# A diffusion trunk's two attentions written as three-part steps, issued on TensorE in a fixed staggered order

## The chip, the cores and the metric

The kernel runs on one core of a Trainium2 chip. The metric is device time in microseconds of one execution. A core has TensorE (PE; its weight loads are listed as PEld), VectorE (DVE), ScalarE (ACT), GpSimd (POOL) and SyncE (SP), which issues the transfers here. Each engine takes its instructions in the order in which they stand in its own queue, and waits on semaphores for the others.

## What is computed

One step of a small diffusion trunk of two layers. 640 tokens go through each layer: 512 latent tokens and 128 prompt tokens. A layer is a feed-forward half step, a mixer and another feed-forward half step. The mixer has three parts on the same input, whose outputs are concatenated and projected: multi-head latent attention (MLA, 8 heads, all keys), window attention with a sink (SWA, 8 query heads on 2 key heads, a band of three blocks of 128 plus 128 cached tokens), and a gated delta network run in both directions (GDN, 4 heads). Prompt tokens attend to the 128 prompt tokens only.

```python
def mla_attend(q_nope, q_rope, k_nope, k_rope, v):
    scale = (MLA_NOPE + MLA_ROPE) ** -0.5
    def one(qs):                       # a block of 128 queries
        qn, qr = qs
        s = (jnp.einsum('bqhd,bshd->bhqs', qn, k_nope)
             + jnp.einsum('bqhr,bsr->bhqs', qr, k_rope)).astype(jnp.float32) * scale
        p = jax.nn.softmax(s, axis=-1).astype(v.dtype)
        return jnp.einsum('bhqs,bshd->bqhd', p, v)
...
def swa_band_attend(q, k, v, k_ctx, v_ctx, sink):
...
    s_loc = jnp.where(valid[None, :, None, None], s_loc, -jnp.inf)
    s_ctx = jnp.einsum('bnqkgd,blkd->bnkgql', qb, k_ctx).astype(jnp.float32) * scale
...
    p = jax.nn.softmax(jnp.concatenate([s_loc, s_ctx, snk], axis=-1), axis=-1)
...
def mixer_latent(h, lp, ctx):
...
    o_gdn, _ = gdn_bidirectional(pr, lp, st_c[:, 0], st_c[:, 1])
    out = jnp.concatenate([o_mla, o_swa, o_gdn], axis=-1) @ lp['w_out']
...
def macaron_layer(x, mod, lp, mix_fn):
    x = x + g1 * (0.5 * swiglu(modulate(rms_norm(x, lp['norm_ffn1']), sh1, sc1), lp['ffn1_w1'], lp['ffn1_w2']))
    m, aux = mix_fn(modulate(rms_norm(x, lp['norm_mix']), sh2, sc2))
    x = x + g2 * m
    x = x + g3 * (0.5 * swiglu(modulate(rms_norm(x, lp['norm_ffn2']), sh3, sc3), lp['ffn2_w1'], lp['ffn2_w2']))
    return x, aux
```

## The kernel before

All of it is float32; large matrix products run as three products of a high and a low part (`linear`, line 104). Activations stand transposed, features on partitions. The mixer of a layer (`mixer`, from line 315) works in this order:

- The input projections and the four GDN heads of the latent tokens (`gdn_group`, groups 0 to 3), then `project`, which makes MLA's queries, keys and values and writes them to DRAM. The four heads of the prompt form a fifth group.
- A GDN group has a preparation: norm sums (line 615), transposes and Gram matrices in PSUM banks of the kind G, a triangular inverse of 16 x 16 blocks on VectorE in 15 dependent rounds (lines 692 to 694), and the block products (line 703), which alternate with VectorE. A scan follows: two directions, eight steps each, of a matmul at line 742, one at line 745, and VectorE's updates (lines 743, 746), in one bank each, S0 and S1.
- Window attention, `swa` (line 946). For a head and a block of 128 queries: scores into an S bank (line 981, masks line 985; the prompt's block line 1006), then `finish` (line 898): the maximum on VectorE (905), the bias (907 or 909), the exponential on ScalarE (910), for SWA the sink's exponential and its sum (912, 913), the reciprocal (914) and the scaling on GpSimd (915). Then `pv` (line 918): 128 x 128 transposes on TensorE into T banks (931), copies by ScalarE (938), products with the values (942), and the output's copy (944). Query blocks go in pairs, since their products share the values.
- MLA, `mla` (line 1011): the same with 640 columns of scores per block (line 1036, six matmuls each), five pairs of transposes and five products of 256 columns per pair of blocks. A head is two pairs and the prompt's block. After head 0 the fifth group's output is normed and written (`tail`, in two pieces).
- After two MLA heads the pool of GDN is given back and the outputs that lie in DRAM are loaded again and split into high and low parts (`osplit`; tile `of`, line 67 on ScalarE). Then come the output projection and the residual.

PSUM has eight banks. During the projections they are L 4, G 2, S0 1, S1 1; in window attention S 2 and T 2 take the place of L, and G, S0 and S1 stay; in MLA S has two tiles of two banks and T four.

The order on every engine is a scheduler's: it simulates the program as it is written and lets each engine take what is ready. So in window attention TensorE's queue mixes scores, transposes and products with the fifth group's preparation and with two scans.

Of the kernel before, what the change touches and what calls it, by code (L numbers as in the profile page):

```python
# [11 lines left out]
AX = mybir.AxisListType  # L12
PSUM = bass.MemoryType.PSUM
# [28 lines left out]
class Net:  # L42
# [272 lines left out]
    def mixer(self, l, A, B, G):  # L315
# [5 lines left out]
        self.enter_banks(G=2, S0=1, S1=1, side="right")  # L321
# [174 lines left out]
        with self.pool("wo") as wp:  # L496
            o = {}

            def osplit(i, f):
                hi = wp.tile([P, T], F32R, tag="o", name=self.nm("oh"), bufs=24)  # L500
                lo = wp.tile([P, T], F32R, tag="o", name=self.nm("ol"), bufs=24)
                self.split(f, hi, lo)
                o[i] = (hi, lo)

            for i in (8, 9, 10, 11, 4, 5, 6, 7, *range(1)):
                f = wp.tile([P, T], F32, tag="of", name=self.nm("of"), bufs=2)
                nc.sync.dma_start(f, self.do[i])
                osplit(i, f)
            self.mla(l, range(2, 8), wp, osplit)
            self.leave_banks()  # L510
            acm.__exit__(None, None, None)
            self.hp_open()
            self.open_x()
            for k in range(KD):
                nc.sync.dma_start(self.x[k], self.xd[k])
            with self.banks(L=6, G=2):
                order = (8, 9, 10, 11, 4, 5, 6, 7, 0, 1, 2, 3)
                for n in range(KD):
                    w = self.weight(a['wo'][l, n, :, 8:], 4, P) + self.weight(a['wo'][l, n, :, :8], 8, P)
                    w = w[:4] + w[8:] + w[4:8]  # L520
                    self.residual(n, w, [o[i] for i in order], G, True)
# [396 lines left out]
    def pv(self, blocks, vv, o, r0, c0, width):  # L918
# [17 lines left out]
        for p, used in tiles:  # L936
            f = self.att.tile([P, 512], F32, tag="pt", name=self.nm("pt"), bufs=6)
            nc.scalar.activation(f[:, :used], p[:, :used], AF.Copy)
            hl.append(f)
        po = self.pt("T")  # L940
# [4 lines left out]

    def swa(self, l):
        nc, att = self.nc, self.att
        sink = self.sm(l, 'sink')
        for kv in range(2):
# [8 lines left out]
            for hh in range(4):  # L958
                head = kv * 4 + hh
                r0 = 64 * (head % 2)  # L960
                if hh % 2 == 0:
                    ot = att.tile([P, T], F32, tag="out", name=self.nm("out"), bufs=2)
                qh = att.tile([P, T], F32R, tag="q", name=self.nm("q"), bufs=4)
                for n in range(2):
                    self.move(qh[64 * n:64 * n + 64], self.dsq[head // 2][n][r0:r0 + 64])
                fin = lambda p, w: self.finish(p[:, :w].unsqueeze(1), SC_SWA, -SC_SWA, self.nsink[:, l * 8 + head:l * 8 + head + 1], sink[:, head:head + 1])

                def scores(n):
                    q = slice(n * P, (n + 1) * P)
                    p = self.pt("S")  # L970
                    lo, hi_ = max(0, n - 1), min(4, n + 2)
                    nl = hi_ - lo
                    if n >= 2:
                        rng = [(0, lo * P, T - lo * P)]
                    else:
                        rng = [(0, 0, nl * P), (nl * P, TL, P)]
                    k = 0
                    last = 2 * len(rng) + (n > 0) + (n < 3)
                    for o0, k0, w in rng:
                        for x in (kh, kl):  # L980
                            nc.tensor.matmul(p[:, o0:o0 + w], lhsT=qh[:, q], rhs=x[:, k0:k0 + w], start=(k == 0), stop=(k == last - 1))  # L981
                            k += 1
                    for on, o0, m in ((n > 0, 0, 'msw1'), (n < 3, (nl - 1) * P, 'msw2')):
                        if on:
                            nc.tensor.matmul(p[:, o0:o0 + P], lhsT=self.identb, rhs=self.mask[m], start=False, stop=(k == last - 1))
                            k += 1
                    return p, (nl + 1) * P, lo, nl

                for pair in range(2):
                    info = []  # L990
                    for n in (2 * pair, 2 * pair + 1):
                        p, w, lo, nl = scores(n)
                        info.append((fin(p, w), lo, nl))
                    blocks = [(4, [(info[j][0], info[j][2] * P, j) for j in range(2)])]
                    single = []
                    for b in range(4):
                        parts = [(info[j][0], (b - info[j][1]) * P, j) for j in range(2)
# [276 lines left out]
```

## Time and profile before

| | us |
|---|---|
| median of three runs (3323.11 to 3327.07) | 3326.66 |
| the profiled execution | 3325.07 |
| its span | 3323.3 |
| window attention, layer 0 (first score to first MLA score) | 111.35 |
| MLA, layer 0 (to the output projection) | 105.64 |
| window attention, layer 1 | 110.00 |
| MLA, layer 1 | 106.63 |

The page lists busy time by engine; a matmul's end is modelled, and short ones overlap, so starts are a better measure of them than durations. A view by stretches gives busy time and the granted clock of TensorE within bounds. A time line lists what an engine ran, neighbours of one kind merged, with the idle time ahead of it in brackets and what ended it.

### The profile page before, as it was taken

To read this page: it belongs to the slowest core of one execution; us is meant where nothing else is said; L and a number is where in the kernel's file an instruction comes from. 1 tells how busy PE (TensorE), PEld (TensorE's weight loads), DVE (VectorE), ACT (ScalarE), POOL (GpSimd) and SP (SyncE) were. 2 spreads that over 40 slices of the span, in tenths; PEclk is the share of its full clock that TensorE was granted. 3 is DMA by queue.
4 is the path that set the end of the run, shared out by engine and by line. 5 is a ranking of instruction groups with operands and counts; after the bars stand their busy time and mean duration, and the time that the engine had idled before them with its cause. 6 is when DMAs were issued, how large, how long until landed. Compare 5 with 4: busy or idle time off the path is not lost.

```text
span 3323.3 us, 56733 instructions
## 1 busy us (share of the span) xinstructions
PE 3241.5 (98%) x22036; PEld 3129.5 (94%) x22036; DVE 1886.3 (57%) x4357; ACT 1384.8 (42%) x3041; POOL 452.2 (14%) x480
## 2 busy tenths in 40 slices
PE   8999999999998999999999999999999989999998
PEld 5999999999887999999999999999998879999998
DVE  4564577686885355643346735477878653433333
ACT  3332334554676433322233323255466763321222
POOL 0000011222343100100000100012114340000000
PEclk9999999999999999999999999999999999999999
DMA  6443453322714224522224534333235242222222
GB/s 212 128 149 116 134 164 127 97 76 91 201 54 138 84 86 133 155 94 72 69 92 143 156 99 139 98 103 110 72 121 152 75 138 74 69 73 74 83 65 76
DMA packets 180190, 364.78 MB, mean 110 GB/s; under 512 B 28112, under 2 KB 68176, under 8 KB 179920
## 3 DMA queue, kind: packets, MB, share of 16 engines
q1 hardware_dynamic: 179920, 361.15, 35.2%
q8 instruction: 173, 2.83, 0.4%
q14 instruction: 97, 0.79, 0.1%
HBM read 315.03 MB, written 46.04 MB: 109 GB/s over the span
## 4 chain that ended last, share of the span: by engine, by line
PE 87%; DVE 6%; ACT 3%; DMA 2%; issue 2%; SPq 0%; POOL 0%; POOLq 0%; DVEq 0%; ACTq 0%
PE psL L104 72%; PE psT L942 3%; PE psG L703 3%; PE psS L1036 2%; PE psT L931 1%; PE psG L275 1%; PE psS L742 1%; DMA of<-do 1%; PE psS L745 1%; ACT pr L910 1%; PE psS L981 1%; DVE hf L169 1%; DMA adaw<-in_wada_dram 0%; DVE wlo L70 0%; PE psS L776 0%
## 5 line engine op out<-in xcount | busy, mean ns | idle before, releaser
L70 DVE TENSOR_TENSOR wlo<-wr,whi 128x512 fp32r<-128x512 f32 (+2 forms) x726 | 494.2, 682 | 709.5 <-ACT whi L67 708.0
L67 ACT ACTIVATE whi<-wr 128x512 fp32r<-128x512 f32 (+2 forms) x726 | 446.2, 616 | 876.2 <-PE psL L104 614.9
L104 PE MATMUL psL<-hb,whi 128*128 128x320 f32 x1968 | 523.8, 313 | 0.7 <-DVE hb L171 0.5
L104 PE MATMUL psL<-hc,whi 128*128 128x320 f32 x1952 | 521.0, 314 | 0.0
L104 PE MATMUL psL<-ha,whi 128*128 128x320 f32 x1856 | 492.3, 312 | 5.0 <-DVE ha L171 3.7
L104 PE MATMUL psL<-hd,whi 128*128 128x320 f32 (+1 forms) x1856 | 486.3, 310 | 1.9 <-DVE hd L171 1.9
L104 PE MATMUL psL<-mh,wlo 128*128 128x320 f32 x1408 | 434.2, 309 | 0.0
L104 PE MATMUL psL<-ml,whi 128*128 128x320 f32 x1408 | 434.0, 309 | 0.0
L104 PE MATMUL psL<-mh,whi 128*128 128x320 f32 x1408 | 432.9, 310 | 0.0
L104 PEld LDWEIGHTS psL<-hb,whi 128*128 128x128 f32 x1968 | 351.9, 189 | 2.6 <-DVE hb L171 1.2
L104 PEld LDWEIGHTS psL<-hc,whi 128*128 128x128 f32 x1952 | 349.4, 189 | 0.8
L104 PEld LDWEIGHTS psL<-ha,whi 128*128 128x128 f32 x1856 | 329.8, 188 | 8.6 <-DVE ha L171 5.7
L104 PEld LDWEIGHTS psL<-hd,whi 128*128 128x128 f32 (+1 forms) x1856 | 328.9, 188 | 5.2 <-DVE hd L171 3.1
L269 DVE SCALAR_TENSOR_TENSOR ada<-adaw,cs,ada 128x512 f32<-128x512 f32 x448 | 313.7, 743 | 0.0
L104 PE MATMUL psL<-hb,wlo 128*128 128x320 f32 (+1 forms) x984 | 307.3, 312 | 0.0
L104 PE MATMUL psL<-hc,wlo 128*128 128x320 f32 (+1 forms) x976 | 305.6, 313 | 0.0
L104 PE MATMUL psL<-hd,wlo 128*128 128x320 f32 (+1 forms) x928 | 287.7, 310 | 0.0
L104 PE MATMUL psL<-ha,wlo 128*128 128x320 f32 (+1 forms) x928 | 287.5, 311 | 0.0
L104 PEld LDWEIGHTS psL<-ml,whi 128*128 128x128 f32 x1408 | 264.0, 188 | 2.8
L104 PEld LDWEIGHTS psL<-mh,whi 128*128 128x128 f32 x1408 | 263.5, 188 | 3.0
L104 PEld LDWEIGHTS psL<-mh,wlo 128*128 128x128 f32 x1408 | 264.1, 188 | 2.0
L273 POOL TENSOR_TENSOR adal<-ada,adah 128x512 fp32r<-128x512 f32 x64 | 89.8, 1404 | 1041.7 <-ACT adah L67 823.3
(299 smaller groups left out, 5612.1 us busy)
## 6 DMA issues: line engine op xcount, KB each, us to landing
adaw<-in_wada_dram SPq DMA_DIRECT2D x288, 256.0 KB, 2.9
wr<-in_w1a_dram SPq DMA_DIRECT2D x88, 512.0 KB, 3.7
wr<-in_w1b_dram SPq DMA_DIRECT2D x88, 512.0 KB, 3.5
wr<-in_win_dram SPq DMA_DIRECT2D x54, 512.0 KB, 3.5
wr<-in_w2a_dram SPq DMA_DIRECT2D x32, 512.0 KB, 4.0
wr<-in_w2b_dram SPq DMA_DIRECT2D x32, 512.0 KB, 3.5
wr<-in_wo_dram SPq DMA_DIRECT2D x16, 512.0 KB, 3.6
dqn<-hd SPq DMA_DIRECT2D x24, 320.0 KB, 3.1
```

What stands on the lines that cost most here:

```text
L67: self.nc.scalar.activation(dst, src, AF.Copy)
L70: self.nc.vector.tensor_tensor(dst, src, hi.bitcast(F32), ALU.subtract)
L104: i = nc.tensor.matmul(p[:m, :cw], lhsT=w[:, :m], rhs=r[:, c0:c0 + cw], start=(k == 0 and n == 0), stop=(k == kt - 1 and n == 2))
L169: nc.vector.scalar_tensor_tensor(t[:, c0:c0 + n], self.x[k][:, s], A[:, k, g:g + 1], r[j][:, c0:c0 + n], ALU.mult, ALU.mult)
L269: nc.vector.scalar_tensor_tensor(acc[g], raw, c, acc[g], ALU.mult, ALU.add)
L273: nc.gpsimd.tensor_tensor(lo, acc[g], hi.bitcast(F32), ALU.subtract)
L275: nc.tensor.matmul(ps[:2, :], lhsT=self.sel[:, g, :], rhs=x, start=(g + n == 0), stop=(g + n == 2))
L703: nc.tensor.matmul(p[:, s], lhsT=lhs[:, s], rhs=rhs[:, s], start=True, stop=True)
L742: nc.tensor.matmul(p1[:, :P], lhsT=qw[:, u, c, 64 * d:64 * d + P], rhs=S, start=True, stop=True)
L745: nc.tensor.matmul(p2[:, :P], lhsT=KD_[d][c][:, us], rhs=UU[d][:, us], start=True, stop=True)
L942: nc.tensor.matmul(po[:, oc:oc + w], lhsT=vv[:, vb, :], rhs=hl[ti][:, s0:s0 + w], start=(n == 0), stop=(n == len(place) - 1))
L1036: nc.tensor.matmul(p[:, j, :w], lhsT=x[:96, qc], rhs=y[:96, k0 + j * w:k0 + j * w + w], start=(i == 0), stop=(i == 2))
```

## The change

Both attentions become lists of steps, each a Python generator that issues in three parts. The first part is the scores of two query blocks (or the prompt's one) and their softmax, the second the transposes and their copies, the third the products. `staged` walks the list: it issues the first part of a step, the second part of the step before, the third part of the one before that. Within it TensorE's instructions keep the order in which they are issued against each other; the other engines stay with the scheduler, and matmuls from outside may be placed between. A head is three steps: pair, prompt, pair. Giving back S0 and S1 and making S wide is a step, and so are the fifth group's norm and output and the reload of outputs. The banks of L and of G are both left ahead of window attention; T has four banks through both attentions, and S two, of one bank in window attention and of two in MLA. MLA's heads 2 to 7 are written as before, each with its loads in its first step.

```diff
-        self.enter_banks(G=2, S0=1, S1=1, side="right")
+        scan = self.banks(S0=1, S1=1, side="right")
+        scan.__enter__()
+        self.enter_banks(G=2, side="right")
         self.enter_banks(L=4)
...
         self.leave_banks()
+        self.leave_banks()
         self.hp_close()
...
-        with self.banks(S=2, T=2):
-            self.swa(l)
-            t = tail("S0", "T")
-            next(t)
-        self.leave_banks()
-        self.enter_banks(S=2, T=4)
-        self.mla(l, range(2), hook=lambda: list(t))
+        o = {}
+        first, last = tail("S0", "T"), []
...
+        def widen():
+            last.pop().__exit__(None, None, None)
+            scan.__exit__(None, None, None)
+            last.append(self.banks(S=2))
+            last[0].__enter__()
+            yield
+            yield
...
+        def collect():
+            self.leave()
+            self.wp = self.enter("wo")
+            for i in (8, 9, 10, 11, 4, 5, 6, 7):
+                fetch(i)
+            yield
+            yield
+            fetch(0)
+
+        steps = [*self.swa(l), norm(), widen(), *self.mla(l, 0), output(), *self.mla(l, 1), collect()]
+        for head in range(2, 8):
+            steps += self.mla(l, head, osplit)
+        with self.banks(T=4):
+            last.append(self.banks(S=2))
+            last[0].__enter__()
+            self.staged(steps)
+            last.pop().__exit__(None, None, None)
...
             nc.scalar.activation(f[:, :used], p[:, :used], AF.Copy)
             hl.append(f)
+        yield
         po = self.pt("T")
...
+    def staged(self, steps):
+        with self.tc.manual_schedule(engines={PE}):
+            one = two = None
+            for step in (*steps, iter(()), iter(())):
+                next(step, None)
+                for g in (one, two):
+                    if g is not None:
+                        next(g, None)
+                one, two = step, one
...
+        return [s for head in range(8) for s in (latent(head, 0), prompt(head), latent(head, 1))]
...
+        def latent(pair):
+            if pair == 0:
+                load()
+            vv, ot = self.pair
+            prs = [fin(n, 0, 2, 320) for n in (2 * pair, 2 * pair + 1)]
+            yield
+            blocks = [(s, [(prs[j], s * P, j) for j in range(2)]) for s in range(5)]
+            yield from self.pv(blocks, vv, ot, r0, pair * 256, 256)
...
+        return [latent(0), prompt(), latent(1)]
```

What this does to TensorE's queue shows at three places.

The start of window attention in layer 0. Before, from the norm sums of the fifth group (`QK`) on; psS_10521 is the first score tile.

```order
L615 MATMUL psG_9517<-ones,QK_9518 128x2 x4
L615 MATMUL psG_9517<-ones,QK_9524 128x2 x4
L634 MATMUL psG_9543<-mats,k_9509 128x128 x4
L745 MATMUL psS_1645_9058<-uu_9035,kd_8841 128x128
L981 MATMUL psS_10521<-k_10508,q_10518 128x256
L981 MATMUL psS_10521<-k_10509,q_10518 128x256
L981 MATMUL psS_10521<-k_10508,q_10518 128x128
L981 MATMUL psS_10521<-k_10509,q_10518 128x128
```

Now the same scores (psS_10530) stand here, behind the last block products (psG) and behind one matmul of each kind of the fifth group's scan (S tiles 1804 and 1805):

```order
L733 MATMUL psG_9764<-TT_9755,U_9727 128x128 x4
L733 MATMUL psG_9773<-TT_9762,ke_9771 128x128 x4
L733 MATMUL psG_9779<-vn_9558,TT_9762 128x128 x4
L772 MATMUL psS_1804_9819<-st_9803,wqb_9511 128x128
L733 MATMUL psG_9788<-TT_9769,ke_9786 128x128 x4
L733 MATMUL psG_9794<-vn_9558,TT_9769 128x128 x4
L775 MATMUL psS_1804_9819<-uu_9784,kd_9590 128x128
L772 MATMUL psS_1805_9825<-st_9807,wqb_9511 128x128
L1032 MATMUL psS_10530<-k_10517,q_10527 128x256
```

Two rows stood between the norm sums and the first score; now 64 do, the whole preparation among them.

MLA, about head 3. Before, between the scores of one pair (psS_12190, some rows above) and the first transpose of that pair (of pr_12181, the last row):

```order
L942 MATMUL psT_12167<-pt_12163,vv_11965 128x256 x2
L1036 MATMUL psS_12232<-k_12107,q_12104 128x128
L1036 MATMUL psS_12232<-k_12113,q_12104 128x128
L1036 MATMUL psS_12232<-k_12107,q_12110 128x128
L1036 MATMUL psS_12271<-k_12259,q_12256 128x320
L1036 MATMUL psS_12271<-k_12265,q_12256 128x320
L1036 MATMUL psS_12271<-k_12259,q_12262 128x320
L1036 MATMUL psS_12271<-k_12259,q_12256 128x320
L1036 MATMUL psS_12271<-k_12265,q_12256 128x320
L1036 MATMUL psS_12271<-k_12259,q_12262 128x320
L942 MATMUL psT_12167<-pt_12165,vv_11965 128x256
L931 MATMUL psT_12206<-mats,pr_12181 128x128
```

Now the last transposes of an older pair (pr_12048, pr_12064), a prompt product, the prompt's scores (psS_12150), and the first transposes of the pair pr_12103 and pr_12119, whose scores were issued just ahead of the older pair's ten transposes:

```order
L961 MATMUL psT_12138<-mats,pr_12048 128x128
L961 MATMUL psT_12138<-mats,pr_12064 128x128
L973 MATMUL psT_12147<-pt_12075,vv_11960 128x128
L1104 MATMUL psS_12150<-k_12087,q_12084 128x128
L1104 MATMUL psS_12150<-k_12093,q_12084 128x128
L1104 MATMUL psS_12150<-k_12087,q_12090 128x128
L961 MATMUL psT_12163<-mats,pr_12103 128x128
L961 MATMUL psT_12163<-mats,pr_12119 128x128
```

Products of an older pair and half of the next pair's scores stood between a pair's scores and its transposes; now a prompt product and the prompt's scores do, beside the older transposes, which stand there in both.

Window attention, about head 4. Before, behind the scores of one pair (psS_11174 and psS_11191), whose transposes come only behind a prompt's:

```order
L931 MATMUL psT_11086<-mats,pr_11052 128x128
L931 MATMUL psT_11086<-mats,pr_11070 128x128 x2
L703 MATMUL psG_9791<-vn_9555,TT_9766 128x128 x4
L942 MATMUL psT_11094<-pt_11090,vv_11035 128x256 x2
L745 MATMUL psS_1803_9816<-uu_9781,kd_9587 128x128
L742 MATMUL psS_1804_9822<-st_9804,wqb_9508 128x128
L981 MATMUL psS_11228<-k_11033,q_11171 128x512
L981 MATMUL psS_11228<-k_11034,q_11171 128x512
L985 LDWEIGHTS identb
L985 MATMUL psS_11228<-bmsw_334,identb 128x128
L985 LDWEIGHTS identb
```

Now behind the scores of one pair (psS_11032 and psS_11049, softmax tiles pr_11038 and pr_11056), from the end of the older pair's seven transposes on:

```order
L961 MATMUL psT_11072<-mats,pr_10983 128x128
L961 MATMUL psT_11072<-mats,pr_10998 128x128
L961 MATMUL psT_11072<-mats,pr_10983 128x128
L973 MATMUL psT_11080<-pt_11011,vv_10519 128x128
L1069 MATMUL psS_11083<-k_11019,q_11029 128x128
L1069 MATMUL psS_11083<-k_11020,q_11029 128x128
L961 MATMUL psT_11097<-mats,pr_11038 128x128
L961 MATMUL psT_11097<-mats,pr_11056 128x128
```

Block products of GDN and scan matmuls are gone from here, and the prompt's scores and one product are what is left ahead of the pair's own transposes.

## Rows read from the trace of the kernel before

**Rows 1.** The page's first part: busy time of each engine, instructions.

```profile
PE 3241.5 (98%) x22036; PEld 3129.5 (94%) x22036; DVE 1886.3 (57%) x4357; ACT 1384.8 (42%) x3041; POOL 452.2 (14%) x480
```

**Rows 2.** Stretches: us; busy of PE, PEld, DVE, ACT, POOL; PE clock; DMA share; GB/s.

```profile
896.00:1007.35 111.35, 104.26 (x722) 92.20 (x723) 87.31 (x328) 80.52 (x251) 46.07 (x54) 0.97 0.28 73
1007.35:1112.99 105.64, 93.89 (x566) 84.29 (x566) 52.70 (x136) 70.63 (x171) 43.85 (x41) 0.95 0.46 135
2532.58:2642.58 110.00, 102.03 (x719) 89.70 (x719) 88.03 (x332) 80.04 (x251) 47.72 (x56) 0.98 0.28 74
2642.58:2749.21 106.63, 94.55 (x566) 84.02 (x566) 51.85 (x132) 70.71 (x171) 42.85 (x40) 0.95 0.46 134
```

**Rows 3.** Time line of TensorE, layer 0: start, duration, what ran [idle before].

```profile
892.01 1.88 PE L615 MATMUL psG<-ones,QK 128*128 128x2 f32 x16
...
896.00 0.75 PE L981 MATMUL psS<-k,q 128*128 128x256 f32 x4 [1.40 <-DMA q<-dsq]
...
948.31 1.95 PE L703 MATMUL psG<-bd,U 128*128 128x128 f32 x16
...
968.16 1.06 PE L703 MATMUL psG<-vn,TT 128*128 128x128 f32 x8
```

**Rows 4.** VectorE, 896 to 941: the stretch, then groups by line (count, busy, mean ns).

```profile
896.00:941.00 45.00, 41.39 (x271) 35.25 (x271) 42.29 (x181) 32.58 (x105) 22.04 (x25) 0.96 0.36 83
...
L905 DVE TENSOR_REDUCE mx<-psS 128x1 f32<-128x384 f32 (+2 forms) x19 | 10.6, 561 | 2.2 <-PE psS L985 1.9 <-PE psS L1006 0.2
...
L913 DVE TENSOR_TENSOR den<-den 128x1 f32<-128x1 f32 x17 | 4.7, 277 | 0.1
...
L907 DVE TENSOR_SCALAR nb<-mx,nsink 128x1 f32<-128x1 f32 x19 | 3.8, 202 | 0.1
...
L914 DVE RECIPROCAL den<-den 128x1 f32<-128x1 f32 x17 | 2.6, 152 | 0.0
```

**Rows 5.** Time line of TensorE: first and last block products of the fourth group.

```profile
874.61 3.00 PE L703 MATMUL psG<-bd,U 128*128 128x128 f32 x24
...
890.89 1.06 PE L703 MATMUL psG<-vn,TT 128*128 128x128 f32 x8
```

**Rows 6.** Time line: first two query blocks of MLA in layer 0, engine by engine.

```profile
1007.35 2.01 PE L1036 MATMUL psS<-k,q 96*128 96x320 f32 x12
...
1008.51 0.82 DVE L905 TENSOR_REDUCE mx<-psS 128x1 f32<-128x640 f32 x1 [0.85 <-PE psS L1036]
...
1011.71 2.46 POOL L915 TENSOR_TENSOR pr<-pr,den 128x640 f32<-128x640 f32 x2 [2.94 <-DVE den L914]
...
1014.05 2.15 PE L931 MATMUL psT<-mats,pr 128*128 128x128 f32 x10
```

**Rows 7.** Groups by line and shape, 880 to 1115: the softmax at 512 columns.

```profile
L915 POOL TENSOR_TENSOR pr<-pr,den 128x512 f32<-128x512 f32 x16 | 16.7, 1045 | 22.3 <-DVE den L914 15.3 <-DVE X L694 3.8 <-DMA k<-dsk 1.7
...
L910 ACT ACTIVATE pr<-psS,nb 128x512 f32<-128x512 f32 x16 | 11.0, 687 | 4.9 <-DVE nb L907 2.0 <-PE psT L931 1.6 <-DVE X L694 1.1
...
L905 DVE TENSOR_REDUCE mx<-psS 128x1 f32<-128x512 f32 x16 | 10.9, 683 | 2.3 <-PE psS L985 2.3
```

**Rows 8.** Time line of TensorE: window scores, their products, and ten transposes.

```profile
908.07 0.77 PE L981 MATMUL psS<-k,q 128*128 128x384 f32 x4
...
908.80 1.74 PE L942 MATMUL psT<-pt,vv 128*128 128x256 f32 x8
...
1105.16 1.25 PE L931 MATMUL psT<-mats,pr 128*128 128x128 f32 x10
```

**Rows 9.** Stretches, columns as in rows 2: a full one, then two behind waits.

```profile
1080.00:1100.00 20.00, 20.00 (x133) 18.63 (x132) 10.73 (x31) 16.03 (x41) 10.29 (x11) 1.00 0.43 137
1035.00:1040.00 5.00, 4.82 (x16) 3.84 (x17) 3.07 (x7) 4.23 (x12) 2.50 (x2) 0.66 0.75 208
1045.00:1050.00 5.00, 3.50 (x25) 3.08 (x23) 2.50 (x5) 1.08 (x3) 1.61 (x2) 1.00 1.03 276
```

**Rows 10.** Waits of ScalarE, 1007 to 1113: us in total, times, longest us.

```profile
ACT oh L67 <- DMA of<-do: 7.6, 4, 2.5
```

More of the change, by code (lines that the diff above doesn't have):

```diff
@@ new lines, in mixer, with norm, output, osplit @@
+        o = {}
+        first, last = tail("S0", "T"), []
+        def norm():
+            next(first)
+            yield
+            yield
+        def output():
+            yield
+            list(first)
+            yield
[6 more added lines that the diff above has]
+            yield
+        def osplit(i, f):
+            hi, lo = (self.wp.tile([P, T], F32R, tag="o", name=self.nm("o"), bufs=24) for _ in range(2))
+            self.split(f, hi, lo)
+            o[i] = (hi, lo)
@@ L948, in swa, with keys @@
         sink = self.sm(l, 'sink')
-        for kv in range(2):
+        K, Q = {}, {}
+        def keys(kv):
             kh, kl = (att.tile([P, 768], F32R, tag="k", name=self.nm("k"), bufs=4) for _ in range(2))
@@ L957, in swa @@
                 self.move(vv[:, :, half], self.dsv[kv])
[L958 to L997, printed above, removed]
-                                 if info[j][1] <= b < info[j][1] + info[j][2]]
-                        if len(parts) == 2:
-                            blocks.append((b, parts))
-                        elif parts:
-                            single.append((b, parts))
-                    self.pv(blocks + single, vv, ot, r0, pair * 256, 256)
-                p = self.pt("S")
-                for n, x in enumerate((kh, kl)):
-                    nc.tensor.matmul(p[:, :P], lhsT=qh[:, TL:], rhs=x[:, T:], start=(n == 0), stop=(n == 1))
-                self.pv([(5, [(fin(p, P), 0, 0)])], vv, ot, r0, TL, P)
-                if hh % 2 == 1:
-                    nc.sync.dma_start(self.do[4 + head // 2], ot)
@@ L1011, in mla, with queries @@
-    def mla(self, l, heads, wp=None, osplit=None, hook=None):
-        nc, a, att = self.nc, self.a, self.att
-        for head in heads:
-            r0 = 64 * (head % 2)
-            rows = slice(r0, r0 + 64)
-            q, k = [], []
+            K[kv] = kh, kl, vv
+        def queries(head):
+            r0 = 64 * (head % 2)
+            if head % 2 == 0:
+                Q[head // 2, 'out'] = att.tile([P, T], F32, tag="out", name=self.nm("out"), bufs=2)
+            qh = att.tile([P, T], F32R, tag="q", name=self.nm("q"), bufs=4)
+            for n in range(2):
+                self.move(qh[64 * n:64 * n + 64], self.dsq[head // 2][n][r0:r0 + 64])
+            Q[head] = qh
@@ new lines, in latent @@
+        def latent(head, pair):
+            if pair == 0:
+                if head % 4 == 0:
+                    keys(head // 4)
+                queries(head)
+            kh, kl, vv = K[head // 4]
+            info = []
+            for n in (2 * pair, 2 * pair + 1):
+                p, w, lo, nl = scores(Q[head], kh, kl, n)
+                info.append((fin(head, p, w), lo, nl))
+            yield
+            blocks = [(4, [(info[j][0], info[j][2] * P, j) for j in range(2)])]
+            single = []
+            for b in range(4):
+                parts = [(info[j][0], (b - info[j][1]) * P, j) for j in range(2)
+                         if info[j][1] <= b < info[j][1] + info[j][2]]
+                if len(parts) == 2:
+                    blocks.append((b, parts))
+                elif parts:
+                    single.append((b, parts))
+            ot = Q[head // 2, 'out']
+            yield from self.pv(blocks + single, vv, ot, 64 * (head % 2), pair * 256, 256)
+            if pair == 1 and head % 2 == 1:
+                nc.sync.dma_start(self.do[4 + head // 2], ot)
```

114 lines of the change are left out of this document (73 added, 41 removed).

## Prediction

> **What bounds the kernel now.** I read the page first: TensorE is busy for 3241.5 of 3323.3 us [rows 1], so only stretches where it waits, or runs slowly, have anything to give. The change touches two such stretches per layer, and one view by stretches prices them [rows 2]: window attention of layer 0 from its first score to the first score of the latent (MLA) attention, 111.35 us, then that attention, 105.64 us; in layer 1 110.00 and 106.63. TensorE is marked busy for 104 and 94 us of the first two, so what perfect order could win is some 20 us per layer, plus what the lower clock costs (0.97 and 0.95 on the mean). The time line then shows what window attention is mixed with: the norm sums of the fifth group of the delta network (the prompt's) run at 892.01, the first score at 896.00, and that group's block products only at 948.31 to 969.2 [rows 3]. So the whole preparation of that group is hidden beside window attention. The profiled execution took 3325.07 us (3323.3 of span), 1.6 under the median of 3326.66; the sum is made against it.
>
> **The change part by part.** Pools and steps move; the arithmetic of every head stays.
>
> *The preparation comes out from under window attention.* The new scores take the two PSUM banks of G, which the fifth group still uses, and the printed order has the first score behind all of that group's block products. What is late next is those products. How long do they take alone? Two pieces. From the norm sums to the first product is 56.3 us before (892.01 to 948.31) [rows 3]. In that time VectorE is the busy engine, 42.29 of 45 us, of which the softmax's four instructions make 10.6 + 4.7 + 3.8 + 2.6 = 21.7 us [rows 4]. They come later now, so I take 56.3 - 21.7 = 34.6 us. The products themselves took 17.3 us for the fourth group, which had no attention beside it (874.61 to 891.95) [rows 5]. So the last product ends at 892.0 + 34.6 + 17.3 = 943.9, its eviction 0.7 later (VectorE's 512 columns, [rows 7]), and the first score runs 944.6 - 896.0 = **49 us later**. Bounds: if nothing is won the end stays at 969.2 and the shift is 74; if the chain is only VectorE's remaining 20.6 us plus the 17.3, it is 34. I take 49, since VectorE had next to no gap there. The transfers of keys and queries, for which the first score waited before, are then hidden by this. The scan of the fourth group also runs in that gap, while the fifth group's scan stays mixed into window attention.
>
> *Window attention with the new order.* A step issues its scores, then the transposes of the step before it, then the products of the one before that, and TensorE takes them in that order. A head is three steps: two query blocks, the prompt (one small score tile), two query blocks. The prompt's step is tiny, and that is the point: behind a head's first scores stand only seven transposes of the older step, one prompt product and two prompt scores, and then the transposes of those very scores. By the trace seven transposes are 0.8 us (0.11 each, from ten in 1.25), and the small pieces some 0.45 (half of a 256-column product's 0.4, and the prompt's scores by their columns) [rows 8]: **cover 1.25 us**. A softmax of 512 columns needs 0.68 (maximum), 0.69 (exponential) and 1.05 (GpSimd's scaling), 2.4 us in sum [rows 7], and between them the bias, the sink's exponential, the reciprocal and the hops; I take 4.0, between that 2.4 and the 4.8 measured below for the wider one. TensorE's own work of a head: scores 2 x 0.73 and 2 x 0.55 (the outer blocks have three quarters of the columns), prompt 0.25, 15 transposes 1.65, products 2 x 1.6 (four in 1.74 with the tail of the last) and 0.2, in all 7.8 us [rows 8]. So a head takes 7.8 - 1.25 + 4.0 = 10.55 us, eight of them 84.4, plus some 5 for start and drain and 2 for scan matmuls that wait in bad places: 91 us against 111.35. **Minus 20 us**; with 2.4 or 4.8 as the wait it would be minus 33 or minus 14.
>
> *MLA with the new order.* Here the chain lies open in the trace of before: twelve score matmuls, six for each of two query blocks, start at 1007.35; the first maximum runs at 1008.51, the two scalings on GpSimd from 1011.71 to 1014.17, and the transposes start at 1014.05 [rows 6]. They end at 1009.36, so the pair needs **4.8 us** from its last score to its last scaled tile. Cover in the new order: ten transposes 1.1, a prompt product 0.2, three prompt scores 0.25, in all 1.55. The work of a head: TensorE ran 133 matmuls in 20.00 us at full clock without a gap [rows 9], and a head has 70 (27 scores, 21 transposes, 22 halves of products), so 10.5 us. A head then takes 10.5 - 1.55 + 4.8 = 13.75 us, eight 110, with start and drain 115, against 105.64 that already hold its own stalls. **Plus 9 us.** The old order had four or five products and half a pair of scores more ahead of those transposes; that is the cover that goes. Ends: with the 2.95 us of the three large instructions 99, with the 7.6 us that ScalarE waited for reloaded outputs [rows 10] on top of 115, 123. The reload becomes a step behind head 1; its loads stand in the SP queue among the keys and queries of the next heads as before, with two buffers, and with ScalarE now idle between exponentials I let that cost nothing more. The fifth group's norm and output steps keep their eight and four matmuls on TensorE and stand in the drain. Four T banks in place of two in window attention are in the 91 us already, which is built from TensorE's work and the wait alone.
>
> *The clock.* Stalls cost twice: from 1035 to 1040, behind a wait of TensorE, the granted clock is 0.66, a mix of 1.2 and 2.4 GHz that loses 5 x 0.34 = 1.7 us of work [rows 9]. The new order has 16 long waits per layer (2.75 us in window attention, some of it filled by the scan, 3.2 in MLA). I take four falls, **plus 7 us**; none is 0, all 27.
> The Trainium skill, page "TensorE: Matmul & The Clock Gate", section "A second HAM failure mode: psum-queue depth-cycling", says that frequent short idles between groups of matmuls make the clock fall and recover again and again. The rows agree that it can; by that rule all 16 would fall, and that is the second rival below.
>
> Sum per layer: 49 - 20 + 9 + 7 = **45 us**, two layers 90: 3325 + 90 = **3415 us**. Nothing before the first attention changes its order, and the feed-forward parts stay as they are.
>
> **The rivals.**
> 1. *The stagger covers the softmax* (faster). Place: the transposes behind the prompt's scores. If the softmax of a pair took no longer than the cover (1.25 and 1.55 us), window attention would take 62.4 + 2 + 6 = 70 and MLA 84 + 6 = 90: 49 - 41 - 16 = -8 per layer, 3309 us. One us off both waits is worth some 18 us per layer, so it decides from waits of about 1.5 and 2.3 us. Against it: three instructions alone need 2.4 and 2.95.
> 2. *The clock falls at every wait*: 27 in place of 7, and the block products, alternating with VectorE, also at half clock, some 10 us: 75 per layer, 3475 us. For it: the row of 1035; against it: from 1045 to 1050 TensorE was busy for 3.50 of 5 us and kept 1.00 [rows 9].
> 3. *The preparation is not bound by VectorE*, so moving the softmax away wins little: shift 70 in place of 49, 3457 us. Against it: 42.29 of 45.
> 4. *All terms small*: shift 36, waits a fifth shorter (-14), no fall of the clock: 11 per layer, 3347 us.
> 5. *It does not do what it says*, the engines being no later than before: 3325. The printed order speaks against it.
>
> **How the numbers follow.** Forecast 0.58, rival 2 0.12, rival 3 0.09, rival 4 0.08, rival 1 0.08, rival 5 0.05. A difference under 0.2% (some 6.6 us) can't be told from none. Faster 0.08, same 0.05, slower 0.87. The range holds the forecast with its bounds, rivals 2 and 3, and half of rival 4: 3350 to 3475 us.
>
> **What would show it.** Right: in the profile of the changed kernel the first score of layer 0 near 945 us, with TensorE half idle from 900 on; the wait of the transposes for GpSimd's scaling (a line hardly seen before) among the longest of TensorE, about 3 us once per head; MLA at 13 to 14 us per head in place of 10.5 to 13.2; VectorE's maximum waiting less behind other work. Wrong: a first score before 930, transposes that wait under 1 us, or MLA under 105 us.

## The result, and the profile after

The changed kernel takes 3484.35 us (median of 4 runs, 3479.74 to 3487.91) against 3324.89 (median of 4) for the kernel before: ratio 1.048, 95% interval 1.0467 to 1.0493, so 159 us slower. The direction was forecast, the size was not: 90 us were forecast, and 3484 lies 9 us outside the range. The profiled execution spans 3482.5 us. Its page, engine totals and granted clock in 40 slices:

```profile
PE 3312.2 (95%) x22036; PEld 3171.4 (91%) x22036; DVE 1890.0 (54%) x4357; ACT 1392.0 (40%) x3041; POOL 452.0 (13%) x480
...
PEclk9999999999888999999999999999998789999999
```

TensorE's marked time is 70.7 us more than in [rows 1], for the same arithmetic, and there are two dips of the clock, one in each layer, where the fifth group's preparation and the two attentions lie. Three stretches of layer 0 (from the norm sums to the first score of window attention, to the first score of MLA, to MLA's last product; busy time and count of each engine, then granted clock, share and rate of the DMA), and MLA of layer 1:

```profile
892.00:947.10 55.10, 42.26 (x249) 36.56 (x247) 40.32 (x143) 18.84 (x54) 13.99 (x14) 0.78 0.28 64
947.10:1055.70 108.60, 90.02 (x498) 74.20 (x499) 53.35 (x197) 64.13 (x199) 35.29 (x42) 0.86 0.17 50
1055.70:1194.60 138.90, 106.44 (x567) 91.59 (x565) 50.07 (x134) 72.49 (x172) 42.58 (x40) 0.89 0.34 103
...
2769.20:2908.50 139.30, 106.26 (x567) 92.11 (x565) 49.89 (x134) 72.59 (x172) 42.66 (x40) 0.89 0.35 103
```

Against [rows 2] the first score comes 51.1 us later (947.1 for 896.0), window attention is 2.8 shorter (108.6 for 111.35), MLA 33.3 longer (138.9 for 105.64): 81.6 us per layer, in layer 1 much the same, and in two layers about the 159. Where is it on TensorE? From 892 to MLA's end the engine was without work for 20 us before (1.4 + 7.1 + 11.8; busy 2.60 of the 4 us ahead of the first score) and is for 64 now (12.8 + 18.6 + 32.5). What the lowered clock costs, reckoned as busy time times one less the granted clock, is 8 us before (3.1 + 4.7) and 33.6 now (9.3 + 12.6 + 11.7). So 44 us of waiting and 26 of half clock; the other 12 are busy time that is marked more at full clock; their cause stays open.

What it waits for, in the two attentions of layer 0 (waits in sum, times, longest), after:

```profile
PE psT L961 <- POOL pr L945: 37.4, 45, 1.4
PE psS L1104 <- ACT pr L940: 8.3, 5, 4.7
PE psS L772 <- DVE st L776: 2.1, 5, 0.8
```

and the same view of the kernel before, from 896 to 1113:

```profile
PE psT L942 <- ACT pt L938: 6.8, 9, 2.9
PE psS L1036 <- ACT pr L910: 3.9, 2, 2.1
```

The transposes (line 961, before 931) now wait for GpSimd's scaling (line 945). Before, they waited for it (then line 915) once in both layers, for 0.2 us. One head of MLA, TensorE's time line (start, duration, line, tiles, count, and in brackets the idle time ahead and who ended it):

```profile
1126.99 2.02 PE L1104 MATMUL psS<-k,q 96*128 96x320 f32 x12
1128.86 0.27 PE L961 MATMUL psT<-mats,pr 128*128 128x128 f32 x1
1129.80 1.20 PE L961 MATMUL psT<-mats,pr 128*128 128x128 f32 x9 [0.67 <-POOL pr L945]
...
1131.14 0.55 PE L1104 MATMUL psS<-k,q 96*128 96x128 f32 x3
1132.67 0.33 PE L961 MATMUL psT<-mats,pr 128*128 128x128 f32 x1 [0.98 <-POOL pr L945]
1133.88 1.20 PE L961 MATMUL psT<-mats,pr 128*128 128x128 f32 x9 [0.88 <-POOL pr L945]
1134.92 4.01 PE L973 MATMUL psT<-pt,vv 128*128 128x256 f32 x10
```

The scores of the first two query blocks end at 1129.0; behind them stand the transposes of the older step, a prompt product and the prompt's scores, as the printed order said, and at 1131.69 TensorE is through. The transposes of the two scaled tiles start at 1132.67 and 1133.88. GpSimd ends the second tile at 1133.83 (1131.37 + 2.46, below), 4.8 us after the last score; counted in the same way, 4.8 was forecast. There is a second wait that the prediction did not have, of 0.67 us at 1129.80, in the transposes of the other pair of blocks. The same softmax on the three other engines:

```profile
1128.17 1.70 DVE L935 TENSOR_REDUCE mx<-psS 128x1 f32<-128x640 f32 x2 [0.17 <-PE psS L1104]
...
1130.12 0.89 ACT L940 ACTIVATE pr<-psS,nb,rq 128x640 f32<-128x640 f32 x1 [1.91 <-DVE nb L939]
...
1131.37 2.46 POOL L945 TENSOR_TENSOR pr<-pr,den 128x640 f32<-128x640 f32 x2 [1.62 <-DVE den L944]
```

Each of the three engines stood waiting for its input before its row, so none is late with other work here. It is the bare chain of maximum, exponential and scaling, and GpSimd's two scalings in a row are half of it. Then comes the clock. In that time line ten products take 4.01 us; in other heads 2.32. In stretches of 2 us, the same place in two heads (columns as above):

```profile
1132.00:1134.00 2.00, 0.44 (x2) 0.25 (x3) 0.27 (x3) 1.95 (x6) 1.83 (x2) 1.00 0.04 8
1134.00:1136.00 2.00, 2.00 (x13) 1.79 (x14) 0.16 (x1) 1.44 (x4) 0.40 (x1) 0.78 0.00 0
1136.00:1138.00 2.00, 2.00 (x6) 1.63 (x5) 0.00 (x0) 0.00 (x0) 0.00 (x0) 0.50 0.00 0
...
1148.00:1150.00 2.00, 0.42 (x2) 0.14 (x1) 0.54 (x3) 2.00 (x8) 2.00 (x2) 1.00 0.00 0
1150.00:1152.00 2.00, 1.73 (x13) 1.65 (x14) 0.16 (x1) 1.32 (x5) 0.62 (x2) 1.00 0.00 0
```

Both heads wait the same 0.98 and 0.88 us (in the second, ahead of 1149.07 and 1150.28). In the first the clock falls to 1.2 GHz (0.50) as the work comes back, in the second it stays at 2.4 (1.00); what decides between the two, these rows do not show. The first head, from prompt scores to prompt scores, takes 16.4 us (1131.14 to 1147.54), the second 14.1 (to 1161.66).

### The profile page after: what moved, and what is told of

Read it like the earlier page. It is cut to its first block, busy times and chain, and to the rows that moved or that the text cites. A ratio compares the mean times of both kernels' runs of the same rounds, so it can differ in the third digit from the quotient of the medians.

```text
span 3482.5 us, 56806 instructions
## 1 busy us (share of the span) xinstructions
PE 3312.2 (95%) x22036; PEld 3171.4 (91%) x22036; DVE 1890.0 (54%) x4357; ACT 1392.0 (40%) x3041; POOL 452.0 (13%) x480
## 3 DMA queue, kind: packets, MB, share of 16 engines
q1 hardware_dynamic: 179920, 361.15, 33.6%
```

## Experiments

Two theories stood against each other. A: the bank plan uncovers the preparation (some 50 us per layer, part of it given back), and in the attentions the fixed order puts too little work between scores and their transposes, so that TensorE waits out the chain, with a half clock behind it. B: one of the parts does it all, the banks or the order. The ratios are against runs of the kernel before on the same chip. Differences between two changed versions can be between chips; on all of them the kernel before took 3324.3 to 3325.5 us.

**The banks alone, on the kernel before.**

```
-        self.enter_banks(G=2, S0=1, S1=1, side="right")
+        scan = self.banks(S0=1, S1=1, side="right")
+        self.enter_banks(G=2, side="right")
...
-        with self.banks(S=2, T=2):
-            self.swa(l)
+        with self.banks(T=4):
+            with self.banks(S=2):
+                self.swa(l)
```

(G is left ahead of window attention.)

> The kernel before with only the new bank plan: the fifth group's two preparation banks are given back ahead of window attention, which then has four T banks; every step keeps its old code and the order that the scheduler gives. Theory A (the bank plan alone costs about 50 us per layer, and shorter window attention without the preparation gives some of it back): first window score near 947 us, window attention 80 to 90 us instead of 111, MLA unchanged at 106, so 20 to 30 us per layer slower: 3365 to 3385 us. Rival B (the fixed order of TensorE makes all of the loss, the banks none): 3315 to 3335 us, with the first score near 896.

Measured: 3358.06 us, ratio 1.0101 (1.0086 to 1.0116): 33 us slower. Its three stretches:

```profile
892.00:950.14 58.14, 46.32 (x274) 40.47 (x272) 41.84 (x145) 19.93 (x56) 14.91 (x16) 0.77 0.31 72
950.14:1026.52 76.38, 73.02 (x499) 62.94 (x499) 52.23 (x198) 60.56 (x198) 34.88 (x42) 1.00 0.24 72
1026.52:1129.56 103.04, 92.73 (x568) 83.36 (x568) 51.49 (x132) 70.98 (x172) 42.84 (x40) 0.97 0.48 139
```

The first score comes 54 us later, and window attention without the preparation in it takes 76.4 us in place of 111.35: 54 - 35 - 2.6 (MLA) = 16.5 per layer. Theory A named the right places and priced them a little too high. The half of B that blames the banks alone falls: they are a fifth of the loss.

**The order alone taken away**: the changed kernel without the line `with self.tc.manual_schedule(engines={PE}):`.

> The changed kernel with the same banks, steps and order of issue, but TensorE's order in both attentions left to the scheduler. Theory A (waits that the fixed order puts in front of the transposes, the half clock behind them): the first score stays near 947, window attention falls from 109 to 85 us, MLA from 139 to 110, so about 50 us per layer less than the changed kernel: 3380 us. Rival C (the loss in the attentions is in the steps and their order of issue on the other engines, not in TensorE's fixed order): 3470 to 3490 us.

Measured: 3365.40 us, 1.0121 (1.0106 to 1.0136), 119 us less than the changed kernel. First score at 947.7, window attention and MLA by stretches:

```profile
947.68:1022.02 74.34, 70.45 (x482) 60.35 (x482) 53.30 (x198) 58.19 (x195) 34.39 (x41) 1.00 0.23 68
1022.02:1135.01 112.99, 100.94 (x586) 89.60 (x585) 51.30 (x133) 72.64 (x175) 44.71 (x41) 0.94 0.45 130
```

So C falls: the steps and their order of issue cost some 7 us over the banks alone, the fixed order of TensorE 119. B's other half falls too, since the banks' 33 us are there without that order.

**The preparation back beside window attention**, fixed order kept: G stays until that attention's end, which has two T banks.

> The changed kernel with the preparation's banks kept until the end of window attention, which has two S and two T banks as before; steps and fixed order stay. Theory A: the first score is back near 896 us and the preparation's products fill part of the waits, window attention takes about 125 us from there in place of 160 (51 of delay and 109), MLA stays at 139: about 35 us per layer faster than the changed kernel, 3415 us. Rival D (preparation and softmax share VectorE, ScalarE and GpSimd, and TensorE in fixed order waits for all of it, so nothing is won): window attention 150 to 160 us, 3470 to 3490 us.

Measured: 3431.36 us, 1.032 (1.0303 to 1.0337): 53 us less than the changed kernel, not the 70 of A and not D's nothing. The first score is back at 898.98, window attention takes 130.0 us (137.9 in layer 1), MLA 137.9. The preparation does run beside window attention under this order, though less well than before.

**One more step of cover**: everything as changed, but transposes two steps behind their scores and products three, and so seven buffers for the scaled tiles in place of five (not in the code below; what the buffers do alone was not run).

```
-                for g in (one, two):
+                for g in (two, three):
...
-                one, two = step, one
+                one, two, three = step, one, two
```

> The changed kernel with transposes two steps behind their scores and products three (in place of one and two), and seven buffers for the scaled tiles in place of five. Theory A (the transposes wait since too little work stands ahead of them): the waits for GpSimd's scaling go, heads fall from 13.6 to about 10 us in window attention and from 14.1 to 16.4 to about 12 in MLA, and the clock stays up: about 45 us per layer, 3395 us. Rival E (two score tiles bound it: the scores of the next step then wait for the exponentials, some 1.5 us per step of two blocks): half of it, 3440 us.

Measured: 3349.33 us, 1.0076 (1.0059 to 1.0094). That is 135 of the 159 us, more than any theory had. Its stretches:

```profile
892.00:945.24 53.24, 41.72 (x240) 35.75 (x240) 39.48 (x141) 18.92 (x54) 13.99 (x14) 0.78 0.29 64
945.24:1018.23 72.99, 70.90 (x491) 61.69 (x491) 51.97 (x194) 59.70 (x197) 34.28 (x41) 1.00 0.25 75
1018.23:1119.89 101.66, 92.63 (x577) 84.52 (x576) 50.85 (x136) 71.33 (x174) 45.22 (x41) 0.98 0.48 141
```

The two longest waits of its TensorE from 945 to 1120:

```profile
PE psS L1104 <- ACT pr L940: 8.5, 7, 2.5
PE psS L1032 <- ACT pr L940: 1.5, 5, 0.4
```

The wait for GpSimd is not shortened but gone; what is left is the wait of rival E, that of the scores for the exponentials. In window attention TensorE is busy for 70.9 of 73 us, with a clock of 1.00. There, with next to no waits, the clock did not fall, so its loss came back together with the waits.

**Work added into the waits**: six matmuls more per step of two blocks, into the bank that the transposes then overwrite.

```
+                if len(blocks) > 1 and len(tiles) == 1:
+                    for _ in range(6):
+                        nc.tensor.matmul(pt, lhsT=self.identb, rhs=..., start=True, stop=True)
```

> The changed kernel with six extra matmuls (bf16, 512 columns, a result that the transposes overwrite) on TensorE ahead of the first transposes of every step of two query blocks: work added into the waits, nothing else changed. Theory F (the half clock behind the waits is a large part of the loss, about 25 us per layer in the two attentions): the engine stays busy, the granted clock stays up, and in spite of 16 times some 1.3 us of added work per layer the kernel is 10 to 20 us per layer faster: about 3455 us. Rival G (the clock is a small part): the added work stands in the way where the waits are shorter than it, 3490 to 3520 us.

Measured: 3445.68 us, 1.0363 (1.0347 to 1.0378), 39 us *less* than the changed kernel. The expectation counted 16 such steps per layer; there are 32, so 192 matmuls more. Six of them on TensorE's time line:

```profile
986.35 1.46 PE L962 MATMUL psT<-bmsw,identb 128*128 128x512 bf16 x6
```

The two attentions of layer 0, by stretches:

```profile
950.74:1047.47 96.73, 93.71 (x594) 72.25 (x595) 55.11 (x197) 63.09 (x199) 35.31 (x42) 1.00 0.20 57
1047.47:1178.80 131.33, 116.23 (x663) 93.57 (x661) 50.56 (x134) 71.80 (x171) 42.65 (x40) 0.96 0.36 109
```

Some 45 us of useless work per layer (by the time line's 0.24 each) make window attention 12 us and MLA 8 us shorter, with a clock of 1.00 and 0.96 for 0.86 and 0.89. The chain over the other engines is as it was, and TensorE has more to do; what it got is the clock. TensorE's waits for the scaling shrink from 37.4 us to 6.7, since the added work stands in them, and the loss to the clock falls from 24.3 us to 4.6 (116.23 us at 0.96). That is theory F, and about what the two attentions got shorter.

**The chain shortened, the cover left**: `nc.vector.tensor_scalar(pr, pr, den[:, 0:1], None, ALU.mult)` in place of GpSimd's multiplication.

> The changed kernel with the division of the weights by their sum on VectorE in place of GpSimd. Theory A (the chain from scores to transposes sets the head): two scalings of 1.25 us in a row on GpSimd become two of 0.4 to 0.8 on VectorE, the chain falls from 5 to about 3.7 us, each head by 1.3 to 2.5, with less half clock: 15 to 30 us per layer, 3430 to 3455 us. Rival J (VectorE takes as long, and the scalings queue behind the next maxima): within 10 us of 3484.

Measured: 3431.70 us, 1.0319 (1.0303 to 1.0334), 53 us less: A's time. A scaling of 640 columns takes VectorE 551 ns where GpSimd took 1253; window attention takes 90.1 us, MLA 131.1. The same edit on the kernel before:

> The kernel before with only the division of the weights on VectorE in place of GpSimd. Theory A (the old order has enough work ahead of the transposes: they waited 0.2 and 0.6 us in sum for GpSimd, so a shorter chain frees nothing there; only the open chain at the start of MLA is shorter): 3312 to 3326 us. Rival K (beside the preparation VectorE is the busy engine, 42 of 45 us, and 40 more instructions on it delay the preparation and the maxima): window attention 5 to 15 us longer per layer, 3335 to 3355 us.

Measured: 3324.54 us, 0.9994 (0.9985 to 1.0004). Worth 53 us under the one order, the edit is worth nothing under the other, where the transposes hardly waited for the scaling. Window attention gained 3 us per layer, MLA lost 5; why MLA lost them stays open.

**The reload.** One head of MLA took 23.6 us (prompt scores from 1076.82 to 1100.46), and in it TensorE waits 4.67 us for the exponential. TensorE's row:

```profile
1100.46 0.90 PE L1104 MATMUL psS<-k,q 96*128 96x128 f32 x3 [4.67 <-ACT pr L940]
```

ScalarE ahead of it:

```profile
1094.03 0.74 ACT L68 ACTIVATE o<-of 128x640 fp32r<-128x640 f32 x1 [0.98 <-DMA of<-do]
...
1095.97 0.74 ACT L68 ACTIVATE o<-of 128x640 fp32r<-128x640 f32 x1 [0.63 <-DMA of<-do]
1098.67 0.74 ACT L68 ACTIVATE o<-of 128x640 fp32r<-128x640 f32 x1 [1.96 <-DMA of<-do]
1099.43 0.89 ACT L940 ACTIVATE pr<-psS,nb,rq 128x640 f32<-128x640 f32 x1
```

The exponential stands in ScalarE's queue behind splits (line 68) that wait for transfers. To spread them, one reload was put behind each of nine steps:

> The changed kernel with the nine outputs that are loaded again not split in one step, but one behind each of the nine steps of heads 2 to 4, each loaded two steps ahead in buffers of its own. Theory H (ScalarE, in its order, waits for those loads with the exponentials queued behind: the head of 23.6 us in place of 14 to 16): MLA 9 us per layer shorter, 3466 us. Rival I (the other waits of that head take the place, or the splits cost the same spread): within 5 us of 3484.

Measured: 3498.67 us, 14 more. It did not do what it was meant to: on ScalarE the splits still stood together, with a wait of 2.52 us for a load among them, and the long wait of TensorE was 2.87 in place of 4.67. Neither theory is tested by it, and where the 14 us come from stays open. So eight of the nine loads were left out and all splits kept:

> The changed kernel with one output loaded again in place of nine; all nine splits take that one tile (this leaves out eight of the reloads, so that what is projected is not the reference's). Theory H (ScalarE waits for the loads, the exponentials behind it, and TensorE for them): the head of 23.6 us falls to 15 to 17, MLA by 7 to 9 us per layer, 3466 to 3471 us. Rival I (the splits themselves or the keys and queries make that head long): within 5 us of 3484.

Measured: 3469.59 us, 1.0437 (1.0421 to 1.0453), 15 less than the changed kernel; MLA 132.0 us for 138.9, window attention of layer 0 108.65 as before. This is H's time: the loads cost 7 us per layer. Its place is only half right: the head of 23.6 us fell to 20.1 and not to 15 to 17, with the nine splits still standing around its exponentials; the other half is in the head behind it, which fell from 14.9 to 11.6.

**In search of a faster version.** Preparation beside, one more step of cover, reloads spread as above:

> Three edits together: the preparation's banks kept beside window attention (two T banks there), transposes two steps behind, the reloads spread over nine steps. Theory A: first score at 896 us, window attention 95 to 110 us with the preparation inside it, MLA 95 us in place of 106, so 5 to 20 us per layer faster than the kernel before: 3285 to 3315 us. Rival D (preparation and softmax hold each other up under a fixed order, as window attention of 130 to 138 us with the banks kept and the shorter stagger suggests): window attention 125 us, 3330 to 3345 us.

Measured: 3335.14 us, 1.0029 (1.0019 to 1.0039). Window attention 115.1 and 120.3 us, MLA 101.4 and 99.6: MLA wins 4 to 7 us against before, window attention loses 4 to 10. That is D's time, with a window attention shorter than D's 125. With the division on VectorE:

> The three edits of the run before last's last kernel (banks kept beside window attention, transposes two steps behind, reloads spread) and the division on VectorE. Theory L (with that cover the chain no longer bounds; what bounds now is the wait of the scores for the exponentials, which the division does not touch): within 8 us of the 3335 without it. Rival A (the chain still bounds window attention beside the preparation): 3305 to 3322 us.

Measured: 3329.34 us, 1.0014 (1.0005 to 1.0023); 6 less, within L's bound of 8. With the order fixed in MLA alone, without and with VectorE:

> The banks kept beside window attention, transposes two steps behind, and TensorE's order fixed in MLA alone; window attention in the same steps is left to the scheduler. Theory A (a fixed order is good where nothing else runs beside it, as the MLA of 101.7 us against 105.9 with the transposes two steps behind, and bad beside the preparation): window attention 105 to 111 us, MLA 100 to 102, so 5 to 10 us per layer less than before: 3305 to 3318 us. Rival M (steps issued in this form and two T banks cost in window attention as much as MLA wins): 3320 to 3335 us.

> The same as the kernel with the order fixed in MLA alone, and the division on VectorE. Theory L: within 8 us of that kernel, since nothing waits for the division any more. Rival K (VectorE is the busy engine beside the preparation): window attention 5 to 15 us longer per layer.

Measured: 3334.73 and 3335.30 us (both 1.0026). M was right: window attention takes 115.8 and 113.6 us with GpSimd, also when left to the scheduler, and MLA 110.2 in layer 0, 101.6 in layer 1. With VectorE the time is the same, as L said. Each step of window attention issued whole, MLA fixed:

> The kernel before's banks and order of issue in window attention, each step issued whole; MLA in steps with a fixed order and transposes two steps behind. Theory A (MLA alone gains by such an order once the cover is longer than the chain): window attention 111 us, MLA 101 to 102 in place of 106: 3314 to 3320 us. Rival M (the start of a fixed order lies open, a drained window attention ahead of it, and that costs the 4 us per layer again): 3322 to 3330 us.

> Old order in window attention with the division on VectorE there, MLA in the fixed order with transposes two steps behind and the division on GpSimd. If both add up: 7 us per layer less than before, 3308 to 3314 us. Rival M (each gain is lost where the two parts meet): 3320 to 3330 us.

Measured: 3546.43 and 3518.59 us (1.0664 and 1.0580). Both missed by some 200 us, and the order is not the old one. MLA took 107 to 110 us, not 101 to 102. In the first of the two, window attention of layer 0 took 215.75 us at a clock of 0.73; the transposes stood right behind their own scores:

```profile
1039.53 0.77 PE L1040 MATMUL psS<-k,q 128*128 128x384 f32 x4
1040.14 0.29 PE L1044 MATMUL psS<-bmsw,identb 128*128 128x128 bf16 x2
1043.02 0.47 PE L964 MATMUL psT<-mats,pr 128*128 128x128 f32 x1 [2.59 <-POOL pr L948]
```

Why the scheduler moved nothing between them here, as it does in the kernel before, is not settled. The run gives, unplanned, a third point for the cover of window attention with the preparation beside it: no step 216 us, one step 130, two steps 115. The point of 216 is under the scheduler's order, the others under the fixed one, so they differ in more than cover. Last, the division on VectorE in the old window attention alone:

> The kernel before with the division on VectorE in window attention alone, on GpSimd in MLA (with it on VectorE in both, window attention took 108.1 and 106.6 us in place of 111.4 and 110.0, and MLA 4.7 more). If the two add up: 3 us per layer less than before, 3317 to 3321 us. Rival (MLA starts with what window attention leaves, so the gain moves): 3322 to 3328 us.

Measured: 3321.45 us, 0.9985 (0.9976 to 0.9995); window attention 108.1 and 106.7 us, MLA 108.3 and 109.6, so most of what the one gained the other lost. The 3 us are too near the limit of what can be told from no change. No version that clearly beats the kernel before was found.

## Why the prediction was right in sign and wrong in size

*The preparation: right, in part by luck.* 49 us were forecast, 51.1 measured, 54 with the banks alone. The pieces:

```profile
931.26 6.64 PE L733 MATMUL psG<-bd,U 128*128 128x128 f32 x32 [3.35 <-ACT bd L740]
...
945.25 1.06 PE L733 MATMUL psG<-vn,TT 128*128 128x128 f32 x8
...
947.10 0.68 PE L1032 MATMUL psS<-k,q 128*128 128x256 f32 x4 [0.29 <-DVE uu L760]
```

The first product came at 931.26 (forecast 926.6), so the chain ahead took 4.6 us more; the products took 15.0 us, 2.3 less than the 17.3 of the forecast. That these two errors met is luck. Nor was TensorE half idle, as the text had it: it is marked busy for 42 of 55 us, and by stretches of 1 us its granted clock was under 0.7 in 24 of them.

*The waits of a head: nearly right.* A head of MLA that keeps its clock takes 14.1 us, 13.75 were forecast; the chain is 4.8 us, as forecast. But two errors meet in the head: its waits are 2.5 us (0.67 + 0.98 + 0.88) for 3.25, and its work is 11.6 us for the 10.5 that were counted from a row of before. In window attention, the last heads:

```profile
1010.82 0.33 PE L961 MATMUL psT<-mats,pr 128*128 128x128 f32 x1 [0.18 <-POOL pr L945]
1012.03 1.37 PE L961 MATMUL psT<-mats,pr 128*128 128x128 f32 x6 [0.88 <-POOL pr L945]
...
1015.78 1.54 PE L961 MATMUL psT<-mats,pr 128*128 128x128 f32 x6 [1.40 <-POOL pr L945]
1017.11 2.66 PE L973 MATMUL psT<-pt,vv 128*128 128x256 f32 x8
```

The waits are 2.5 us per head, 2.75 were forecast, though they lie before two steps, not one. But the head takes 13.6 us and not 10.55, and nearly all of the difference is the clock: eight products take 2.66 us here and 1.68 at 1020.81, and all pieces of this head that follow a wait take some 2.8 us more in sum.

*The clock: the step that failed.* "I take four falls, plus 7 us." By stretches of 1 us the granted clock fell 11 times in the attentions of layer 0 and twice in the preparation; the attentions lose 24.3 us, some 2.2 per fall where 1.7 were taken, the preparation 9.3. So the term of the clock was under a third of its measured size, in the number of falls above all. The row of 1045 [rows 9], in which a pause left the clock at 1.00, was taken for the rule. Both happen: the heads of 1132 and 1148 above have the same waits. Rival 2, which priced a fall at every wait at 27 us and the block products at 10, gave 3475 us and had 0.12; it was the nearest of all, 9 us off. Its 27 us for the attentions are close to the 24.3; its 10 for the block products did not come, as the preparation was only 2.1 us longer than forecast, so the nearness of the whole is in part luck. The Trainium skill (page "TensorE: Matmul & The Clock Gate", section "A second HAM failure mode: psum-queue depth-cycling") tells of a kernel in which frequent short idles between groups of matmuls make the clock go down and up again and again. The trace agrees, with 11 falls, but not every wait brought one.

*The reload: the second step that failed, taken at nothing.* "I let that cost nothing more": the loads cost 7 us per layer, by the run without them. The 7.6 us of ScalarE [rows 10] were in view and named as an end; they were put aside since ScalarE was idle between exponentials, but the time line above has an exponential queued behind them, and TensorE waiting for it.

The errors per layer: the preparation +2.1; window attention without its clock 108.6 - 12.6 = 96.0 for 91, +5.0; MLA without its clock 138.9 - 11.7 = 127.2 for 115, +12.2, of which 6.9 the loads; the clock 24.3 for 7, +17.3. In sum 36.6, and 45 + 36.6 = 81.6, as measured. The 5.0 in window attention and the 5.3 that the loads leave of MLA's 12.2 are not split further.

*What gave the sign.* Three rows named for it came true: first score near 945, transposes that wait for the scaling for 1.1 to 1.9 us ahead of a step, MLA at 14 us per head and more. Rival 1 (the stagger covers the softmax) fell by those rows; the kernel with one more step shows from where it would have decided: there the chain is covered, and the loss is down to 24 us, less than the banks alone cost.

## What to carry to other kernels

An order fixed by hand needs more work between a producer's matmuls and its consumer's than the whole chain over the other engines takes; count that cover at its thinnest step, since the smallest step (here the prompt's) sets it. Waits on TensorE can be paid a second time, at half clock behind them: here 51 us without work in two attentions came with 24 us of clock. Price that into the forecast, and do not take one undisturbed row, in which the clock did not fall, for the rule. Freeing a resource early, here two PSUM banks, also makes the work that held it stand alone; look at what ran beside it first.

## What the runs showed of the hardware that was not expected

Adding 192 matmuls per layer, some 45 us of work, into the waits made the kernel's time 39 us shorter over both layers, with the granted clock in window attention up from 0.86 to 1.00. The same two waits of 0.98 and 0.88 us were followed in one head by 1.2 GHz and in the next by 2.4 GHz. And a division by a per-row number takes GpSimd 1253 ns for 640 columns and VectorE 551.
